# First w_ada tiles ahead of x, context reductions behind the image's, scale and shift on GpSimd, in a hybrid attention and convolution layer

## The chip, the cores and the metric

The kernel runs on one core of one Trainium2 chip. A core has a matrix engine (TensorE, PE in the profile), a vector engine (VectorE, DVE), an activation engine (ScalarE, ACT), a general engine (GpSimd, POOL) and an engine that mostly issues transfers (SyncE, SP). Each runs its own list of instructions in order, and they wait for each other by semaphores. The metric is the time of one execution on the device in microseconds, lower is better. The kernel before took 1092.82 us in the median of three runs (1089.09 to 1093.6).

## The reference

The layer takes 1024 latent tokens x and 256 context tokens ctx of width 1024. The change lies in the first lines, the modulation:

```python
def modulate(x, cond, norm_g, w_ada, b_ada):
    shift, scale, gate = jnp.split(jax.nn.silu(cond) @ w_ada + b_ada, 3, axis=-1)
    return rms_norm(x, norm_g) * (1 + scale) + shift, gate

def hybrid_layer(x, xc, c, c_ctx, lp, update_ctx):     # update_ctx is False: one layer
    h, gate = modulate(x, c, ...)                      # image: conditioned on c
    hc, gate_c = modulate(xc, c_ctx, ...)              # context: conditioned on c_ctx
    z = h @ lp['w_in']                                 # 1024 x 8704
    kc, vc = na_kv(hc @ lp['w_in'][:, A_K:A_Z], ...)   # keys and values of the context
    q, k, v = ...                                      # from z
    ya = neighbourhood_attention(q, k, v, kc, vc, rpb) * silu(z[A_Z])
    yb = short_conv_branch(z, ...)
    yc = conformer_branch(z, ...)
    return x + gate * merge_branches(z, ya, yb, yc, ...)
```

So each of the 1024 columns has a scale and a shift, each of them one dot product of length 1024 with a row of w_ada; one pair for the image (with silu(c)), another for the context (with silu(c_ctx)), from the same rows of w_ada. Everything is float32, and a matrix product is made as three products of rounded parts (high by high, high by low, low by high).

## The kernel before

The 1024 columns are eight blocks of 128, k = 0 to 7. Scale and shift of a block lie in A_t and B_t, one value per partition. They are made on VectorE: a tile `wada` holds 128 rows of w_ada (128 x 1024, 512 KB), and one scalar_tensor_tensor instruction multiplies it by the condition's row and adds up each partition (the function image_ada, line 399; below a *reduction*). Each block has two such tiles, one for the scale and one for the shift, sixteen in all, loaded by load_w_ada (line 346). Two small VectorE instructions then make A_t (line 401) and B_t (line 402) from the sums. The same tiles are reduced a second time with the context's condition row (ctx_ada, line 408), sixteen more reductions.

The opening of the program is one loop over k. In step k: the 384 columns of w_in for the first pair of heads are loaded (`wraw`, line 445), block k's w_ada tiles are loaded and reduced, the weights are split into a high part `wh` (ScalarE, line 450) and a low part `wl` (VectorE, line 452), and `modulated` turns tokens 0 to 511 of block k into `ha`: TensorE transposes four tiles of x into a bank of PSUM (line 371), ScalarE writes the high part with scale and shift applied (line 373) and the same unrounded as `xh` (line 376), and VectorE subtracts to get the low part (line 379). `outer` then adds block k's twelve products per four token tiles to the banks in PSUM (lines 418 to 420). Three steps later, `second` does the same for tokens 512 to 767, into `hb`. There are two banks for transposes, and a bank is free again when its `xh` is written.

x tiles are normalised in `normed`: ScalarE squares and sums (line 358), GpSimd makes the reciprocal root in two instructions (lines 80 and 81), and VectorE (line 363) or ScalarE (line 361) scales the tile. After the loop, rest_image does tokens 768 to 1023, the context's A and B are completed on GpSimd (lines 484 to 486), and context_h transposes and modulates the context tokens. The rows of the first gated unit's weights (`grow`, lines 431 to 433) are loaded and split when k reaches GATED.

Where buffers lie matters for the order. The six w_ada tiles of blocks 0 to 2 (EARLY) lie in buffers that become hb2 to hb7 later, so both reductions must have read a tile before the hb tile that takes its place is written; the table CTX_ROWS puts those six context reductions into steps 4 to 7. The other ten lie in fifteen shared row buffers (ROWS), with x, context and weight tiles.

The order of instructions on each engine is not the order of the code alone. A planner in the language lays the recorded instructions out in time by its own estimates and sorts each engine's list by that; `issue_after` holds an instruction behind another. So a change in the opening moves instructions later in the program too.

```python
def image_ada(k):
    for j in range(2):
        dve.scalar_tensor_tensor(out=junk, in0=wa[k][j], scalar=1.0, in1=sc, ..., accum_out=da[:, j : j + 1])
    dve.tensor_scalar(out=A_t[:, k, 0:1], ...)
    state["ada"] = dve.tensor_scalar(out=B_t[:, k, 0:1], ...)
```

Of the kernel before, what the change touches and what calls it, by code (L numbers as in the profile page):

```python
# [40 lines left out]
GATED = 6  # L41
CTX_AT = (8, 3, 3, 3)

CTX_ROWS = {5: 4, 4: 5, 3: 6, 2: 7, 1: 7, 0: 7}
# [3 lines left out]
def tile_hybrid(ctx: ExitStack, tc, x, xT, cx, cond, crow, ng, w_ada, b_ada, wqkv, wz,  # L48
# [234 lines left out]
    A_t = cst.tile([P, KT, 2], F32, name="A_t")  # L283
    state["vc"] = 0
    B_t = cst.tile([P, KT, 2], F32, name="B_t")
# [22 lines left out]
    with tc.tile_pool(name="st", bufs=1) as st, tc.tile_pool(name="ps_t", bufs=1, space=PSUM) as pst:  # L308
# [17 lines left out]
        cst.tile([P, KT, 2], F32, name="sig")  # L326
# [39 lines left out]
        def modulated(k, tiles, i, hi, lo, on=act, sub=dve):  # L366
# [5 lines left out]
            a, b = A_t[:, k, i : i + 1], B_t[:, k, i : i + 1]  # L372
# [11 lines left out]
        b1 = cst.tile([P, KT], F32, name="b1")  # L384
        pool.tensor_scalar(out=b1, in0=b_t[:, 8:16], scalar1=1.0, scalar2=None, op0=ALU.add)
        x0 = [load_x(x, t, four(a1.tile([P, D], F32, tag=("qT", "kT", "vb")[t], name="xt")) if t < 3 else four(row4k("xt"))) for t in range(4)]
        wa = [load_w_ada(0)]
# [7 lines left out]
        def image_ada(k):  # L395
            junk = st.tile([P, 2, 2, 256], BF16, tag="junk", name="junk", bufs=1)
            da = small[:, 20 + 2 * k : 22 + 2 * k]
            for j in range(2):
                dve.scalar_tensor_tensor(out=junk, in0=wa[k][j], scalar=1.0, in1=sc, op0=ALU.mult, op1=ALU.mult,
                                         accum_out=da[:, j : j + 1])  # L400
            dve.tensor_scalar(out=A_t[:, k, 0:1], in0=da[:, 0:1], scalar1=b1[:, k : k + 1], scalar2=ng_t[:, k : k + 1], op0=ALU.add, op1=ALU.mult)
            state["ada"] = dve.tensor_scalar(out=B_t[:, k, 0:1], in0=da[:, 1:2], scalar1=b_t[:, k : k + 1], scalar2=None, op0=ALU.add)

        def ctx_ada(i):

            k, j = i // 2, i % 2
            junk = st.tile([P, 2, 2, 256], BF16, tag="junk", name="junk", bufs=1)
            dve.scalar_tensor_tensor(out=junk, in0=wa[k][j], scalar=1.0, in1=scx, op0=ALU.mult, op1=ALU.mult, accum_out=dx[:, k, j : j + 1])
# [34 lines left out]
        for k in range(KT):  # L443
# [11 lines left out]
            with tc.issue_after(state["ada"].ins):  # L455
                for i in CTX_ROWS:
                    if CTX_ROWS[i] == k:
                        ctx_ada(i)
            if k == 1:
                x1 += [normed(load_x(x, t, four(row4k("xt"))), act) for t in (4, 5)]  # L460
            if k >= LAG:
                second(k - LAG)
            if k == GATED:
                gated.append(load_rows(wz[CGL], [a1.tile([P, 2, 256], F32R, tag="cht", name="grow", bufs=4) for _ in range(4)]))
            if k == KT - 1:
                x2 = [normed(load_x(x, t, four(row4k("xt"))), act) for t in (6, 7)]
        for k in range(KT - LAG, KT):
            second(k)
        late = [i ^ 1 for i in range(2 * KT) if i ^ 1 not in CTX_ROWS]
# [1049 lines left out]
```

## Time and profile before

| what | value |
|---|---|
| timed runs | 1092.82, 1089.09, 1093.6 us |
| the profiled execution: its own time, its span | 1091.25 us, 1089.5 us |
| TensorE busy | 1064.1 us, 98% of the span |
| VectorE, ScalarE, GpSimd busy | 760.9, 564.5, 633.8 us |
| mean granted TensorE clock | 0.992 |
| moved by DMA | 186.26 MB, mean 171 GB/s |
| image reductions (line 399) | 16, the first at 11.8, the last at 47.9 us, 1217 ns each |
| context reductions (line 408) | 16, the first at 33.6, the last at 76.6 us, 1216 ns each |

A row of an order of time gives the start in us, the duration in us, the engine, the line, the operation, the tiles written and read with their shape, and how often; in brackets the idle time of the engine before it and what ended it. "SPq" is the issue of a transfer by SyncE. PEld is the loading of weights into TensorE, which overlaps with matmuls. A row of the table by stages gives start and end, the length, the busy time of each engine with the number of instructions, the granted clock of TensorE (1.00 is full), the share of time in which the DMA engines were busy, and GB/s.

### The profile page before, as it was taken

What the parts mean: (1) busy time and instruction counts of PE and PEld (TensorE: products, weight loads), DVE (VectorE), ACT (ScalarE), POOL (GpSimd) and SP (SyncE); (2) the same over time, 40 slices, a digit from 0 to 9 for tenths busy, and PEclk for the clock granted to TensorE, in tenths of its full rate; (3) what the DMA queues carried; (4) which work ended last, traced back from release to release, by engine and by line L of the source; (5) the groups of instructions that cost most, each with busy time, mean ns of one, the idle gap of its engine ahead of it and who ended that gap; (6) DMA issues with size and microseconds to landing.
All of it is one profiled execution on the core that took longest, in us unless ns stands there. A gap on an engine that the chain in (4) does not pass through costs nothing.

```text
span 1089.5 us, 16045 instructions
## 1 busy us (share of the span) xinstructions
PE 1064.1 (98%) x5270; PEld 910.6 (84%) x5270; DVE 760.9 (70%) x1261; ACT 564.5 (52%) x1194; POOL 633.8 (58%) x660
## 2 busy tenths in 40 slices
PE   7899999999999999999999999999999999999998
PEld 5788998998999888887888888887888888888886
DVE  6985476666666654433995898997973569988664
ACT  6764676557656675665533334234445534425730
POOL 3154967427646388333998786886685461623770
PEclk7999999999999999999999999999999999999999
DMA  9627514313222346448746446555554998461372
GB/s 349 228 78 244 188 52 126 97 45 106 95 73 77 108 156 215 154 146 299 251 155 191 157 143 190 185 197 193 165 172 160 329 340 303 136 248 62 98 231 97
DMA packets 92995, 186.26 MB, mean 171 GB/s; under 512 B 11792, under 2 KB 36752, under 8 KB 92816
## 3 DMA queue, kind: packets, MB, share of 16 engines
q1 hardware_dynamic: 88304, 183.13, 50.2%
q10 hardware_dynamic: 4608, 2.10, 0.7%
q8 instruction: 42, 0.69, 0.3%
q14 instruction: 41, 0.34, 0.1%
HBM read 136.96 MB, written 50.79 MB: 172 GB/s over the span
## 4 chain that ended last, share of the span: by engine, by line
PE 74%; DMA 7%; DVE 6%; POOL 6%; issue 3%; ACT 2%; SPq 1%; ACTq 0%; POOLq 0%; DVEq 0%
PE ops L110 4%; PE ops L109 4%; PE ops L111 4%; PE qps L678 3%; PE py L635 3%; PE qps L680 3%; PE qps L679 3%; PE pp L615 3%; PE ps L111 3%; PE ps L109 3%; PE ps L110 2%; DVE cv L830 2%; DMA wada<-in_w_ada 2%; PE gd L854 2%; PE gd L855 2%
## 5 line engine op out<-in xcount | busy, mean ns | idle before, releaser
L830 DVE SCALAR_TENSOR_TENSOR cv<-upad,cf_t,cv 128x1024 f32<-128x1024 f32 x120 | 153.8, 1281 | 1.0
L92 POOL TENSOR_TENSOR wl<-wr,wh 128x384 fp32r<-128x384 f32 (+1 forms) x87 | 84.3, 977 | 68.4 <-ACT wh L90 50.7
L764 POOL TENSOR_TENSOR wl<-s,wh 128x512 fp32r<-128x512 f32 x83 | 107.8, 1311 | 17.9 <-ACT wh L763 17.8
L763 ACT CAST wh<-s 128x512 fp32r<-128x512 f32 x111 | 66.3, 610 | 99.8 <-POOL s L767 37.6
L618 DVE TENSOR_TENSOR plo<-pp,phi 128x256 fp32r<-128x256 f32 (+2 forms) x96 | 54.5, 576 | 36.2 <-ACT phi L617 35.3
L90 ACT CAST wh<-wr 128x384 fp32r<-128x384 f32 (+1 forms) x96 | 45.9, 485 | 37.9 <-PE qps L679 16.5
L678 PE MATMUL qps<-ha,wh 128*128 128x512 f32 x160 | 63.1, 396 | 1.6 <-ACT quarter L685 1.6
L679 PE MATMUL qps<-ha,wh 128*128 128x512 f32 x160 | 63.8, 398 | 0.0
L680 PE MATMUL qps<-ha,wl 128*128 128x512 f32 x160 | 62.7, 394 | 0.0
L574 POOL TENSOR_TENSOR bias<-mk,img 64x96 f32<-64x96 bf16 (+1 forms) x96 | 44.7, 472 | 26.5 <-DVE mn L600 19.3
L617 ACT CAST phi<-pp 128x256 fp32r<-128x256 f32 (+2 forms) x96 | 46.5, 495 | 20.4 <-PE pp L615 19.9
L600 DVE CUSTOM_DVE_ANT_0 pt<-sl,bias,mn 128x384 f32<-128x384 f32 (+1 forms) x64 | 37.2, 581 | 17.2 <-PE sl L597 16.2
L764 POOL TENSOR_TENSOR wl<-wro,wh 128x512 fp32r<-128x512 f32 x12 | 16.6, 1384 | 53.6 <-ACT wh L763 53.6
L615 PE MATMUL pp<-ident,pt 128*128 128x128 f32 x304 | 46.9, 272 | 0.0
L80 POOL TENSOR_SCALAR ssh<-ssh 128x4 f32<-128x4 f32 (+1 forms) x40 | 11.5, 287 | 60.5 <-DVE ssh L255 57.7
L601 ACT ACTIVATE pt<-sc,mn 128x256 f32<-128x256 f32 x64 | 30.6, 478 | 30.8 <-DVE mn L600 29.0
L615 PEld LDWEIGHTS pp<-ident,pt 128*128 128x128 f32 x304 | 37.9, 140 | 7.8 <-DVE plo L618 0.3
L81 POOL TENSOR_TENSOR ssh<-ssh,half_neg 128x4 f32<-128x4 f32 (+1 forms) x40 | 39.0, 975 | 3.0
L109 PE MATMUL ps<-wh,hb 128*128 128x384 f32 x112 | 38.8, 347 | 0.6 <-ACT rawc L224 0.5
L608 DVE TENSOR_SCALAR pt<-pt,mn 128x640 f32<-128x640 f32 (+1 forms) x64 | 38.5, 643 | 1.0
L854 PE MATMUL gd<-hb,wh 128*128 128x512 f32 x96 | 37.4, 390 | 1.7 <-DVE c L860 1.7
L111 PE MATMUL ps<-wh,hb 128*128 128x384 f32 x112 | 37.8, 342 | 0.3 <-DVE hb L379 0.3
(437 smaller groups left out, 3753.4 us busy)
## 6 DMA issues: line engine op xcount, KB each, us to landing
wr<-in_wz SPq DMA_DIRECT2D x34, 512.0 KB, 3.8
gs<-gd SPq DMA_DIRECT2D x24, 512.0 KB, 5.3
wr<-in_wz SPq DMA_DIRECT2D x52, 192.0 KB, 2.6
wada<-in_w_ada SPq DMA_DIRECT2D x16, 512.0 KB, 8.6
wrf<-in_wo SPq DMA_DIRECT2D x16, 512.0 KB, 3.5
cht<-chd SPq DMA_DIRECT2D x24, 256.0 KB, 2.9
wro<-in_wout SPq DMA_DIRECT2D x24, 256.0 KB, 4.6
p1d<-quarter SPq DMA_DIRECT2D x20, 256.0 KB, 2.8
```

The lines of the kernel that those rows point to most:

```text
L92: lo_eng.tensor_tensor(out=lo[:, :n], in0=raw[:, :n], in1=hi[:, :n].bitcast(F32), op=ALU.subtract)
L109: pe.matmul(ps, ah, bh, start=i == 0, stop=False)
L110: pe.matmul(ps, ah, bl, start=False, stop=False)
L111: pe.matmul(ps, al, bh, start=False, stop=i == n - 1)
L615: pe.transpose(out=pp[:, c * P : c * P + P], in_=src, identity=ident)
L678: pe.matmul(ps, wh, bh, start=k == 0, stop=False, skip_group_check=True)
L679: pe.matmul(ps, wh, bl, start=False, stop=False, skip_group_check=True)
L680: pe.matmul(ps, wl, bh, start=False, stop=k % 4 == 3, skip_group_check=True)
L763: act.copy(hi, src)
L764: eng.tensor_tensor(out=lo, in0=src, in1=hi.bitcast(F32), op=ALU.subtract)
L830: dve.scalar_tensor_tensor(out=acc, in0=src, scalar=cf_t[:, i, j : j + 1], in1=acc, op0=ALU.mult, op1=ALU.add)
L854: pe.matmul(ps, wh, bh, start=first and j == 0, stop=False, skip_group_check=True)
```

## The change

Three things are changed, and their surroundings with them.

- The first two w_ada tiles are loaded ahead of the first four tiles of x, instead of behind them.
- All sixteen context reductions are recorded after rest_image, held behind the last image reduction. The six tiles whose buffers become hb tiles are loaded a second time, into row buffers; the table CTX_ROWS goes. GATED is 7 instead of 6, and x tiles 6 and 7 are asked for ahead of the `grow` rows.
- A_t and B_t become one tile AB. Per block, GpSimd adds the biases to both sums and multiplies both by their factors (the scale's is the norm's weight, the shift's is 1.0), two instructions on 128x2 in place of two VectorE instructions on 128x1. The constants for it lie in the new tile `ab`. For the context, two GpSimd instructions on 128x16 replace three on 128x8. The tile `var` of a later stage moves into `small`.

```diff
-GATED = 6
+GATED = 7
-CTX_ROWS = {5: 4, 4: 5, 3: 6, 2: 7, 1: 7, 0: 7}
...
+        pool.tensor_copy(ab[:, 0, :, 1:2], b_t[:, :8].rearrange("p (k o) -> p k o", o=1))
+        pool.tensor_scalar(out=ab[:, 0, :, 0:1], in0=b_t[:, 8:16].rearrange("p (k o) -> p k o", o=1), scalar1=1.0, scalar2=None, op0=ALU.add)
+        pool.tensor_copy(ab[:, 1, :, 0:1], ng_t.rearrange("p (k o) -> p k o", o=1))
+        pool.memset(ab[:, 1, :, 1:2], 1.0)
+        wa = [load_w_ada(0)]
         x0 = [load_x(x, t, ...) for t in range(4)]
-        wa = [load_w_ada(0)]
...
             for j in range(2):
-                dve.scalar_tensor_tensor(out=junk, in0=wa[k][j], ..., in1=sc, ..., accum_out=da[:, j : j + 1])
-            dve.tensor_scalar(out=A_t[:, k, 0:1], in0=da[:, 0:1], scalar1=b1[:, k : k + 1], scalar2=ng_t[:, k : k + 1], op0=ALU.add, op1=ALU.mult)
-            state["ada"] = dve.tensor_scalar(out=B_t[:, k, 0:1], in0=da[:, 1:2], scalar1=b_t[:, k : k + 1], scalar2=None, op0=ALU.add)
+                state["ada"] = dve.scalar_tensor_tensor(out=junk, in0=wa[k][j], ..., in1=sc, ..., accum_out=da[:, j : j + 1])
+            pool.tensor_tensor(out=da, in0=da, in1=ab[:, 0, k], op=ALU.add)
+            pool.tensor_tensor(out=AB[:, 0, k], in0=da, in1=ab[:, 1, k], op=ALU.mult)
 
         def ctx_ada(i):
             k, j = i // 2, i % 2
+            if i < EARLY:
+                w = four(row4k("wada"))
+                nc.sync.dma_start(w, four(w_ada[1 - j, k]))
+            else:
+                w = wa[k][j]
...
-            with tc.issue_after(state["ada"].ins):
-                for i in CTX_ROWS:
-                    if CTX_ROWS[i] == k:
-                        ctx_ada(i)
...
-        late = [i ^ 1 for i in range(2 * KT) if i ^ 1 not in CTX_ROWS]
+        late = [*range(EARLY, 2 * KT), *range(EARLY)]
...
         rest_image()
+        with tc.issue_after(state["ada"].ins):
+            for i in late:
+                ctx_ada(i)
...
-        pool.tensor_tensor(out=A_t[:, :, 1], in0=dx[:, :, 0], in1=b1, op=ALU.add)
-        pool.tensor_tensor(out=A_t[:, :, 1], in0=A_t[:, :, 1], in1=ng_t, op=ALU.mult)
-        pool.tensor_tensor(out=B_t[:, :, 1], in0=dx[:, :, 1], in1=b_t[:, :8], op=ALU.add)
+        pool.tensor_tensor(out=dx, in0=dx, in1=ab[:, 0], op=ALU.add)
+        pool.tensor_tensor(out=AB[:, 1], in0=dx, in1=ab[:, 1], op=ALU.mult)
```

Lines of the changed kernel are a few less than before: its image reduction is line 398, its context reduction 412, the two GpSimd instructions 400 and 401, the subtraction 376, the high part 370.

Three places show how the order moves. The first is SyncE's list at the start of the program; `xt` are tiles of x. Before:

```order
L74 DMA cond_t<-in_cond 128x16
L74 DMA ng_t<-in_ng 128x8
L74 DMA b_t<-in_b_ada 128x24
L351 DMA xt<-in_x 128x1024 x4
L346 DMA wada<-in_w_ada 128x1024 x2
L445 DMA wraw<-in_wqkv 128x384 x2
```

and with the change:

```order
L72 DMA cond_t<-in_cond 128x16
L72 DMA ng_t<-in_ng 128x8
L72 DMA b_t<-in_b_ada 128x24
L343 DMA wada<-in_w_ada 128x1024 x2
L348 DMA xt<-in_x 128x1024 x4
L449 DMA wraw<-in_wqkv 128x384 x2
```

The two w_ada tiles and the four x tiles have changed places.

The second is VectorE at the last block, k = 7: `sc` is the image's condition row, `sc1` the context's, ha6 is the output of k = 6, hb3 that of the second half at k = 3. Before:

```order
L399 SCALAR_TENSOR_TENSOR junk_620,pad0_79<-wada_616,sc_200 128x1024
L379 TENSOR_TENSOR ha6_167<-xh_563,ha6_167 128x512
L399 SCALAR_TENSOR_TENSOR junk_620,pad0_79<-wada_618,sc_200 128x1024
L401 TENSOR_SCALAR A_t_175<-pad0_79,b1_217,ng_t_213 128x1
L379 TENSOR_TENSOR hb3_580<-xh_585,hb3_580 128x256
L402 TENSOR_SCALAR B_t_176<-pad0_79,b_t_215 128x1
L452 TENSOR_TENSOR wl_626<-wraw_614,wh_625 128x384
L408 SCALAR_TENSOR_TENSOR junk_650,pad0_79<-wada_304,sc1_231 128x1024
L433 TENSOR_TENSOR grow_597<-wr_610,grow_595 128x256
L408 SCALAR_TENSOR_TENSOR junk_652,pad0_79<-wada_229,sc1_231 128x1024
```

and with the change:

```order
L398 SCALAR_TENSOR_TENSOR junk_595,pad0_79<-wada_591,sc_199 128x1024
L456 TENSOR_TENSOR wl_551<-wraw_539,wh_550 128x384
L376 TENSOR_TENSOR ha6_167<-xh_560,ha6_167 128x512
L398 SCALAR_TENSOR_TENSOR junk_595,pad0_79<-wada_593,sc_199 128x1024
L376 TENSOR_TENSOR hb3_575<-xh_580,hb3_575 128x256
L412 SCALAR_TENSOR_TENSOR junk_777,pad0_79<-wada_391,sc1_232 128x1024
L437 TENSOR_TENSOR grow_655<-wr_657,grow_653 128x256
L472 TENSOR_SCALAR qg8_159<-qg_t_715 128x1
L473 TENSOR_SCALAR kgn_160<-kg_t_717 128x1
L412 SCALAR_TENSOR_TENSOR junk_779,pad0_79<-wada_393,sc1_232 128x1024
L437 TENSOR_TENSOR grow_655<-wr_661,grow_653 128x256
L412 SCALAR_TENSOR_TENSOR junk_781,pad0_79<-wada_441,sc1_232 128x1024
```

A_t and B_t are gone from the list, and the context reductions (line 412) begin only behind the last image reduction; before, three stood ahead of it.

The third is ScalarE between the output of k = 6 and that of k = 7 (ha6 and ha7). Before:

```order
L373 ACTIVATE ha6_167<-xT_ps_557,B_t_176,A_t_175 128x512
L376 ACTIVATE xh_563<-xT_ps_557,B_t_176,A_t_175 128x512
L376 ACTIVATE xh_585<-xT_ps_581,B_t_176,A_t_175 128x256
L361 ACTIVATE xt_670<-xt_670,pad0_79 128x1024
L450 CAST wh_625<-wraw_614 128x384
L432 CAST grow_595<-wr_610 128x256
L361 ACTIVATE xt_677<-xt_677,pad0_79 128x1024
L373 ACTIVATE ha7_168<-xT_ps_629,B_t_176,A_t_175 128x512
```

and with the change:

```order
L370 ACTIVATE ha6_167<-xT_ps_554,AB_175 128x512
L373 ACTIVATE xh_560<-xT_ps_554,AB_175 128x512
L370 ACTIVATE hb3_575<-xT_ps_576,AB_175 128x256
L373 ACTIVATE xh_580<-xT_ps_576,AB_175 128x256
L355 ACTIVATE sq_641,pad0_79<-xt_639 128x1024
L355 ACTIVATE sq_648,pad0_79<-xt_646 128x1024
L436 CAST grow_653<-wr_657 128x256
L370 ACTIVATE hb4_625<-xT_ps_626,AB_175 128x256
L358 ACTIVATE xt_639<-xt_639,pad0_79 128x1024
L436 CAST grow_653<-wr_661 128x256
L370 ACTIVATE ha7_168<-xT_ps_604,AB_175 128x512
```

The squares of x tiles 6 and 7 and the output hb4 now stand ahead of ha7; one of the two scalings and the cast of the weights stand behind it.

More of the change, by code (lines that the diff above doesn't have):

```diff
@@ L282, in tile_hybrid @@
     a1 = a1ctx.enter_context(tc.tile_pool(name="a1", bufs=1))
-    A_t = cst.tile([P, KT, 2], F32, name="A_t")
+    AB = cst.tile([P, 2, KT, 2], F32, name="AB")
     state["vc"] = 0
-    B_t = cst.tile([P, KT, 2], F32, name="B_t")
     def glu(i):
@@ L325, in tile_hybrid @@
         cond_t = const(cond, [P, KT, 2], "cond_t")
-        cst.tile([P, KT, 2], F32, name="sig")
+        ab = cst.tile([P, 2, KT, 2], F32, name="ab")
         act.activation(cond_t, cond_t, AF.Silu)
@@ L371, in modulated @@
                 pe.transpose(out=pt[:, j * P : (j + 1) * P], in_=xt[:, k // 4, k % 4 // 2, k % 2 * P : k % 2 * P + P], identity=ident)
-            a, b = A_t[:, k, i : i + 1], B_t[:, k, i : i + 1]
+            a, b = AB[:, i, k, 0:1], AB[:, i, k, 1:2]
             act.activation(hi, pt[:, :n], AF.Identity, bias=b, scale=a)
@@ L398, in image_ada @@
             for j in range(2):
[L399 to L402, printed above, removed]
+                state["ada"] = dve.scalar_tensor_tensor(out=junk, in0=wa[k][j], scalar=1.0, in1=sc, op0=ALU.mult, op1=ALU.mult,
+                                                        accum_out=da[:, j : j + 1])
+            pool.tensor_tensor(out=da, in0=da, in1=ab[:, 0, k], op=ALU.add)
+            pool.tensor_tensor(out=AB[:, 0, k], in0=da, in1=ab[:, 1, k], op=ALU.mult)
         def ctx_ada(i):
             k, j = i // 2, i % 2
+            if i < EARLY:
[3 more added lines that the diff above has]
+                w = wa[k][j]
             junk = st.tile([P, 2, 2, 256], BF16, tag="junk", name="junk", bufs=1)
-            dve.scalar_tensor_tensor(out=junk, in0=wa[k][j], scalar=1.0, in1=scx, op0=ALU.mult, op1=ALU.mult, accum_out=dx[:, k, j : j + 1])
+            dve.scalar_tensor_tensor(out=junk, in0=w, scalar=1.0, in1=scx, op0=ALU.mult, op1=ALU.mult, accum_out=dx[:, k, j : j + 1])
         image_ada(0)
@@ L1251, in norm_steps @@
         yield from col_sums(square, sums)
-        var = cst.tile([P, KT], F32, name="var")
+        var = small[:, :KT]
         for b in range(2):
```

9 lines of the change are left out of this document (2 added, 7 removed).

## The prediction

> **What bounds the kernel now.** The table by stages was read first, to see where TensorE is not the bound; then, inside the stage that has idle time, the order of time on VectorE, ScalarE and GpSimd, and the queue of SyncE for when tiles land.
>
> ```profile
> PE 1064.1 (98%) x5270; PEld 910.6 (84%) x5270; DVE 760.9 (70%) x1261; ACT 564.5 (52%) x1194; POOL 633.8 (58%) x660
> ```
>
> ```profile
> core 0: us, PE busy (x) PEld busy (x) DVE busy (x) ACT busy (x) POOL busy (x), PEclk, DMA share, GB/s
> 17.00:34.00 17.00, 15.49 (x73) 14.06 (x74) 15.42 (x34) 13.04 (x22) 2.86 (x4) 0.82 1.03 401
> 34.00:51.20 17.20, 13.63 (x72) 12.07 (x70) 17.20 (x39) 12.92 (x25) 3.74 (x5) 0.90 0.56 188
> 51.20:67.00 15.80, 14.50 (x75) 12.77 (x76) 13.86 (x31) 12.53 (x27) 9.41 (x11) 1.00 0.42 144
> 67.00:85.00 18.00, 17.45 (x103) 15.56 (x102) 13.79 (x33) 9.87 (x22) 6.47 (x12) 1.00 0.03 8
> 120.00:1089.50 969.50, 959.69 (x4726) 818.95 (x4724) 674.76 (x1088) 488.49 (x1043) 582.77 (x579) 1.00 0.50 165
> ```
>
> From 120 us on TensorE is busy 959.7 of 969.5 us, so nothing the change does can be won or lost there but by the order of that work. The change acts in the opening. From 17 to 67 us TensorE idles 1.5 + 3.6 + 1.3 = 6.4 us, and VectorE is the bound: 17.20 of 17.20 us busy between 34 and 51.2. TensorE's granted clock is 0.82 and 0.90 there; after a gap of 2.04 us it ran at half pace:
>
> ```profile
> 39.63 0.45 PE L418 MATMUL ps<-wh,ha 128*128 128x384 f32 x1 [2.04 <-ACT ha L373]
> 39.91 0.34 PE L419 MATMUL ps<-wl,ha 128*128 128x384 f32 x1
> 40.31 0.52 PE L419 MATMUL ps<-wl,ha 128*128 128x384 f32 x1
> 43.67 0.34 PE L419 MATMUL ps<-wl,hb 128*128 128x384 f32 x1
> ```
>
> Between 40.31 and 43.67 matmuls start 0.32 us apart instead of 0.17: about 1.7 us lost. The ceiling of the change is so about 6.4 + 1.7 = 8 us.
>
> The last of the eight steps (k = 7) on VectorE:
>
> ```profile
> 44.90 1.22 DVE L408 SCALAR_TENSOR_TENSOR junk<-wada,sc 128x1024 bf16<-128x1024 f32 x1
> ...
> 46.17 1.22 DVE L399 SCALAR_TENSOR_TENSOR junk<-wada,sc 128x1024 bf16<-128x1024 f32 x1
> 47.31 0.08 DVE L399 DVE_READ_ACCUMULATOR junk<-wada,sc 128x1 f32 x1
> 47.31 0.69 DVE L379 TENSOR_TENSOR ha<-xh,ha 128x512 fp32r<-128x512 f32 x1
> 47.92 1.22 DVE L399 SCALAR_TENSOR_TENSOR junk<-wada,sc 128x1024 bf16<-128x1024 f32 x1
> 49.06 0.27 DVE L401 TENSOR_SCALAR A_t<-pad,b,ng_t 128x1 f32<-128x1 f32 x1
> 49.25 0.42 DVE L379 TENSOR_TENSOR hb<-xh,hb 128x256 fp32r<-128x256 f32 x1
> 49.58 0.21 DVE L402 TENSOR_SCALAR B_t<-pad,b_t 128x1 f32<-128x1 f32 x1
> 49.70 0.55 DVE L452 TENSOR_TENSOR wl<-wraw,wh 128x384 fp32r<-128x384 f32 x1
> ```
>
> Starts count, since durations overlap: a reduction holds VectorE 1.15 us, the 512-wide subtraction 0.6, the 256-wide 0.34, A_t 0.19, B_t 0.12, wl 0.48. The tile that L399 reads at 47.92 had long landed: SyncE holds eight transfers, and an issue starts when the one eight before it has landed. The second tile of k = 7 stands eight ahead of cs_t:
>
> ```profile
> 6.10 1.43 SPq L346 DMA_DIRECT2D wada<-in_w_ada  x2
> ...
> 11.05 0.33 SPq L445 DMA_DIRECT2D wraw<-in_wqkv  x1
> 12.36 0.83 SPq L346 DMA_DIRECT2D wada<-in_w_ada  x2
> ...
> 38.78 0.33 SPq L74 DMA_DIRECT2D cs_t<-in_cs  x1
> ```
>
> So it was there by 38.8. By the same rule x tile 0 landed by 6.10 and the two first w_ada tiles by 11.05 and 12.36, five tiles after it: 1.25 us a tile.
>
> **The two w_ada tiles ahead of x.** They now land by about 7.2, the four x tiles by 8.6 to 12.4, two slots (2.5 us) later. ScalarE squares x as it lands:
>
> ```profile
> 11.12 1.06 ACT L358 ACTIVATE sq<-xt 128x1024 bf16<-128x1024 f32 x1
> ...
> 16.16 0.78 ACT L373 ACTIVATE ha<-xT_ps,B_t,A_t 128x512 fp32r<-128x512 f32 x1 [2.26 <-DVE B_t L402]
> ```
>
> The last square starts after three others (1.05 each) and two copies of scx (0.5 each) from 8.6 on: 12.75 instead of 11.12. Behind it come GpSimd's root, VectorE's scaling, the transposes; then k = 0's first output, which before waited for B_t until 16.16 and no longer does. I carry VectorE's first free moment for k = 1 from 16.44 to 17.25 (+0.8) and the first output from 16.16 to 17.65 (+1.5).
>
> **A and B on GpSimd.** VectorE loses eight times 0.19 + 0.12 = 2.5 us of work. But each pair now crosses to GpSimd and back as two dependent operations, and GpSimd does not work freely beside VectorE:
>
> ```profile
> 58.15 1.21 DVE L408 SCALAR_TENSOR_TENSOR junk<-wada,sc 128x1024 bf16<-128x1024 f32 x1
> 58.33 1.10 POOL L80 TENSOR_SCALAR ssh<-ssh 128x4 f32<-128x4 f32 x1 [3.02 <-DVE ssh L255]
> ...
> 62.34 0.20 POOL L80 TENSOR_SCALAR ssh<-ssh 128x4 f32<-128x4 f32 x1
> ...
> 76.25 0.21 POOL L486 TENSOR_TENSOR B_t<-pad,b_t 128x8 f32<-128x8 f32 x1 [2.51 <-DVE junk L408]
> ```
>
> The same L80 takes 0.20 us alone and 1.10 under a reduction, ending when it ends. So each of the pair costs 0.2 at best and up to 1.2 behind the VectorE instruction in flight; the pair 0.5 to 2.4, where B_t was there 0.3 after the reduction. The price is paid where VectorE must wait for the result, at the ha subtraction: pair, then ScalarE's ha and xh (1.4 us). By the new order, filled with these durations, VectorE waits about 1.9 us at k = 1 and at k = 2 (there also for ScalarE, whose scaling of x tiles 4 and 5 needs roots that are held up the same way) and 0.5 each at k = 4 and 5: 4.9, against 1.4 before. I take the blocked value, since VectorE is busy nearly all the time; bounds are 2.3 and 6.5.
>
> A rule of the Trainium skill speaks against this part: "GPSIMD Engine Reference", Specifications, says GpSimd shares its SBUF interfaces with VectorE and contends with instructions that have two SBUF inputs or run in a two-port mode; the reductions and subtractions are such, and the trace agrees (1.10 us against 0.20). By that rule the sum is the one with 4.9 us of waits; without it, 2.3.
>
> **Context rows behind the image's.** Three context reductions (3 x 1.15 = 3.45 us) leave the stretch before the last image reduction, and with GATED = 7 three grow subtractions (1.0). Sum on VectorE at the end of the last image reduction, 49.14 before: -2.5 - 3.45 - 1.0 + (4.9 - 1.4) + 0.8 = -2.65, so 46.5.
>
> **What is late next.** That gain does not reach k = 7's output. ScalarE's order now puts two squares of x tiles 6 and 7 (1.05 each), one scaling (1.1), two grow casts (0.35), and three 256-wide outputs (0.46) ahead of it: 5.25 us after k = 6's xh, which ends at 44.9. And GpSimd's pair for k = 7 stands behind x tile 6's root, which two context reductions hold up. Both give 50.2 to 50.4:
>
> ```profile
> 47.55 1.16 ACT L361 ACTIVATE xt<-xt,pad 128x1024 f32<-128x1024 f32 x1
> ...
> 50.35 0.77 ACT L373 ACTIVATE ha<-xT_ps,B_t,A_t 128x512 fp32r<-128x512 f32 x1
> ...
> 51.18 0.44 PE L418 MATMUL ps<-wh,ha 128*128 128x384 f32 x1 [0.83 <-ACT ha L373]
> ```
>
> On TensorE: it comes to its wait for k = 7 at about 49.75 instead of 51.18 (-1.4), with four matmuls and two transposes of k = 4's second half done that came later before (-0.9). It then waits some 3.1 us in all for k = 7's output and for subtractions queued behind three context reductions, where 1.95 were lost before (+1.15). Further on the hb7 subtraction stands behind nine context reductions and comes at 61.0, when TensorE stands at 59.3 (+1.7). Sum: -1.4 - 0.9 + 1.15 + 1.7 = +0.55.
>
> **The context itself.** After the last image reduction VectorE has 16 context reductions ahead instead of 13 and ends them at about 78.5:
>
> ```profile
> 76.56 1.20 DVE L408 SCALAR_TENSOR_TENSOR junk<-wada,sc 128x1024 bf16<-128x1024 f32 x1
> ...
> 78.25 0.26 POOL L485 TENSOR_TENSOR A_t<-A_t,ng_t 128x8 f32<-128x8 f32 x1
> ...
> 79.45 0.56 ACT L373 ACTIVATE ch<-xT_ps,B_t,A_t 128x256 fp32r<-128x256 f32 x1
> ```
>
> Before, they ended at 77.7, A was there at 78.5 and first used at 79.45. Now it is there at 79.3 to 79.7: I add nothing, bound +1. The **six reloads** are 3 MB, 7.5 us at 1.25 a tile; they fall where the DMA engines idle and are read as the last six reductions, from 66 us on; cover gone, they would cost up to those 7.5:
>
> ```profile
> 45.00:55.00 10.00, 7.67 (x42) 6.40 (x41) 9.63 (x21) 9.59 (x17) 3.26 (x4) 1.00 0.21 66
> ```
>
> In SyncE's queue they stand ahead of the context x and w1raw loads, needed near 63 and 68. The merged tiles and var in small cost nothing.
>
> **Sum.** The profiled execution took 1091.25, its span 1089.5; the three timed runs were 1092.82, 1089.09 and 1093.6. The mean of the four is 1091.7; plus 0.5 gives 1092.2 as the time of a run: no change. (A measurement of this kernel tells about 0.5%, 5.4 us, from no change.)
>
> **Rivals.** *Faster: the relief of VectorE goes through.* If the pairs slip in between VectorE's instructions, waits are 2.3 (-2.6), the later x costs nothing (-1.5), hb7's wait (-1.7) and the 1.15 vanish: 1092.2 - 7 = 1085.2. For it: VectorE is the full bound from 34 to 51 us, and two operations of 0.2 us are cheap. Against: rows of 1.10, and ScalarE's new order. Chance 0.21.
>
> *Slower: the context becomes late.* Sixteen reductions now follow the image, six of them on tiles that SyncE issues only once a row buffer is free, in turn with other loads. The output pairs of the context occupy both transposing banks, so TensorE stops once A and B come later than about 79.5, one for one. With the reloads' 7.5 us uncovered by half, and one more slow stretch of the clock (1.7) at a gap over 2 us: 1092.2 + 3.8 + 1.7 = 1097.7. Against: 20 us between the issue and the first use. Chance 0.13.
>
> *The order of the rest decides.* The planner also rearranges the work after 120 us; TensorE idles 9.8 us there, and half of it more or less would be 1087 or 1097. For: the rows of later stages do differ. Against: TensorE is 99% busy in any order. Chance 0.08, half each way.
>
> *The reloads or the new order do not do what they say:* the forecast then stands anyway.
>
> **How the numbers follow.** Forecast 0.58, faster 0.21, slower 0.13, order 0.08. Some of the forecast's own spread (1088 to 1096) and of the rivals lies inside 0.5%. Faster 0.22, same 0.61, slower 0.17. The range must reach toward 1085 and toward 1098: 1085 to 1098.5 leaves out about 2 in 10.
>
> **What would show it.** Right: the last image reduction ends near 46.5, k = 7's output stays near 50.4, GpSimd's pairs show operations of about 1 us, TensorE waits at hb4 and hb7, TensorE's idle time from 17 to 85 us stays within 2 us of before. Wrong: k = 7's output before 48 (the pairs are cheap, or ScalarE is freer), context A after 82, or TensorE's idle time after 120 us off by more than 3 us.

## The result, and the profile after

The changed kernel took 1085.06 us in the median of seven runs (1083.6 to 1087.99), the kernel before beside it 1091.28 (seven runs, 1087.82 to 1093.6): a ratio of 0.9949, with a 95% interval of 0.9933 to 0.9965. Measured again later, twelve runs against twenty of the kernel before on one chip, it was 0.9961 (0.9947 to 0.9975), 1084.85 against 1089.30. So the change makes the kernel 4 to 6 us faster, at the edge of what I had called no change. The forecast of 1092.2 was too high, mostly by a gain that lies where the forecast had put nothing. One run of the kernel context_only below took 1182.59 us at a granted clock of 0.846, where its others show 0.99; it does not count in that kernel's median, 1088.17.

The profiled execution of the changed kernel is the slowest of its seven runs (1087.99 us, span 1086.2), so its span is only 3.3 us shorter than that of before. Its page begins:

```profile
PE 1063.0 (98%) x5270; PEld 910.3 (84%) x5270; DVE 768.6 (71%) x1245; ACT 563.5 (52%) x1194; POOL 646.2 (59%) x678
```

The table by stages of the changed kernel, with the same stages as in the prediction:

```profile
core 0: us, PE busy (x) PEld busy (x) DVE busy (x) ACT busy (x) POOL busy (x), PEclk, DMA share, GB/s
17.00:34.00 17.00, 12.25 (x53) 10.78 (x54) 13.49 (x22) 11.34 (x18) 6.84 (x11) 0.77 1.03 405
34.00:51.20 17.20, 15.85 (x96) 14.57 (x95) 16.18 (x34) 14.00 (x26) 6.38 (x12) 1.00 0.58 201
51.20:67.00 15.80, 15.29 (x73) 13.34 (x74) 14.83 (x32) 12.35 (x27) 5.74 (x8) 0.89 0.92 320
67.00:85.00 18.00, 17.69 (x100) 15.45 (x99) 14.87 (x33) 11.16 (x25) 12.33 (x15) 1.00 0.05 15
120.00:1086.20 966.20, 958.42 (x4728) 819.45 (x4726) 684.72 (x1088) 487.70 (x1044) 584.98 (x580) 1.00 0.48 165
```

The first stage lost (TensorE 12.25 us busy against 15.49, 53 products against 73), the second won it back (15.85 against 13.63, 96 products against 72, with the clock at 1.00 against 0.90). TensorE's idle time over the four stages from 17 to 85 us is 6.9 us before and after. VectorE is no longer the full bound: 16.18 of 17.20 instead of 17.20. After 120 us the stage is 3.3 us shorter: TensorE idles 7.8 us instead of 9.8, and is busy 1.3 us less (958.42 against 959.69).

The rows that answer the prediction's, on VectorE, ScalarE, GpSimd and TensorE of the changed kernel in order of time:

```profile
45.60 1.22 DVE L398 SCALAR_TENSOR_TENSOR junk<-wada,sc 128x1024 bf16<-128x1024 f32 x1
```

```profile
18.51 0.78 ACT L370 ACTIVATE ha<-xT_ps,AB 128x512 fp32r<-128x512 f32 x1 [2.95 <-PE xT_ps L368]
...
50.19 0.78 ACT L370 ACTIVATE ha<-xT_ps,AB 128x512 fp32r<-128x512 f32 x1
```

```profile
31.84 1.06 POOL L401 TENSOR_TENSOR AB<-pad,ab 128x2 f32<-128x2 f32 x1
...
39.88 0.26 POOL L401 TENSOR_TENSOR AB<-pad,ab 128x2 f32<-128x2 f32 x1
...
47.30 1.41 POOL L79 TENSOR_TENSOR pad<-pad,half_neg 128x1 f32<-128x1 f32 x1
48.68 0.22 POOL L400 TENSOR_TENSOR pad<-pad,ab 128x2 f32<-128x2 f32 x1
48.98 1.18 POOL L401 TENSOR_TENSOR AB<-pad,ab 128x2 f32<-128x2 f32 x1
```

```profile
51.69 1.15 PE L368 MATMUL xT_ps<-ident,xt 128*128 128x128 f32 x4 [1.81 <-ACT xh L373]
```

The last image reduction ends at 46.82 (forecast 46.5, before 49.14). The output of k = 7 starts at 50.19 (forecast 50.2 to 50.4, before 50.35): GpSimd's pair for k = 7 stands behind the root of an x tile, as forecast, and its second operation is stretched to 1.18 us. The first output of all comes at 18.51, later than the forecast 17.65.

Where is the gain, then? The first scores of the attention (the matmuls that write `sl`) mark the end of the opening, the last of them the end of the attention. The view of one source line gives the first and the last start (before, then after):

```profile
L596 PE MATMUL sl<-ks,qd x64: 278/334/443, 114.0 to 475.9; 128*128 128x384 f32 x48, 128*128 128x256 f32 x16
```

```profile
L595 PE MATMUL sl<-ks,qd x64: 277/334/442, 114.3 to 473.7; 128*128 128x384 f32 x48, 128*128 128x256 f32 x16
```

The opening, the only place that the change touches in the code apart from `var`, ends 0.3 us later. The attention takes 359.4 us instead of 361.9. The 2.5 us lie behind the opening, in code that was not changed, only ordered anew.

### The profile page after: what moved, and what is told of

Read it like the earlier page. It is cut to its first block, busy times and chain, and to the rows that moved or that the text cites. A ratio compares the mean times of both kernels' runs of the same rounds, so it can differ in the third digit from the quotient of the medians.

```text
span 1086.2 us, 16054 instructions
## 1 busy us (share of the span) xinstructions
PE 1063.0 (98%) x5270; PEld 910.3 (84%) x5270; DVE 768.6 (71%) x1245; ACT 563.5 (52%) x1194; POOL 646.2 (59%) x678
## 4 chain that ended last, share of the span: by engine, by line
PE 80%; DVE 3%; DMA 1%; POOL 1%; issue 1%; ACT 1%; SPq 0%; ACTq 0%; POOLq 0%; DVEq 0%
PE ops L109 4%; PE ops L107 4%; PE ops L108 4%; PE qps L677 3%; PE qps L678 3%; PE qps L679 3%; PE gd L853 3%; PE gd L855 3%; PE gd L854 3%; PE py L634 3%; PE pp L614 3%; PE ps L107 2%; PE ps L109 2%; PE ps L108 2%; PE ge L855 2%; PE gc L855 2%
## 5 line engine op out<-in xcount | busy, mean ns | idle before, releaser
L79 POOL TENSOR_TENSOR ssh<-ssh,half_neg 128x4 f32<-128x4 f32 (+1 forms) x40 | 43.1, 1078 | 2.9
L607 DVE TENSOR_SCALAR pt<-pt,mn 128x640 f32<-128x640 f32 (+1 forms) x64 | 44.0, 728 | 1.0
```

## The experiments

**Theory and rival.** Theory: the opening is about even, and the gain comes from the planner's other order of the rest. Rival: the three edits bring it themselves, by relieving VectorE.

Comparing the two lists instruction by instruction showed how the orders differ. From the first scores on, the kernel before and the changed kernel part at one place: one pair of VectorE instructions, near 132 us, has changed places. Behind it the lists are sorted differently, TensorE's from 135 to 525 us and VectorE's to 563 us of the kernel before; from there to the end they are the same again, so "the rest" is in fact the attention and a little beyond it. Other small edits of the opening give one of the same two orders of the rest, call them B (as before) and A (as after). So the order could be switched by one edge on that pair with the opening untouched.

### before_pair_swapped and after_pair_swapped

```diff
 # before_pair_swapped: the kernel before, order A
-    def norm(ps, dst, n):
+    def norm(ps, dst, n, after=None):
...
-        dve.tensor_tensor(out=dst..., op=ALU.mult)
+        with tc.issue_after(after) if after else ExitStack():
+            dve.tensor_tensor(out=dst..., op=ALU.mult)
...
-                norm(raw[:, :256], tm, 4)
+                norm(raw[:, :256], tm, 4, state["mn"][1].ins if (hp, t) == (1, 1) else None)
...
-            dve.tensor_reduce(out=mn[:, 0:2], in_=sc, axis=AX.X, op=ALU.min)
+            state.setdefault("mn", []).append(dve.tensor_reduce(out=mn[:, 0:2], in_=sc, axis=AX.X, op=ALU.min))
```

> The kernel before, with one NoSync edge: VectorE's third scaling of raw q and k rows of the second head pair (L257, at 132.46 us in the profile before) is queued behind the row minimum of the second pair of query blocks (L589, at 132.80) and so changes places with it. Nothing ahead of 132 us is touched. From there on the planner's order is that of the changed kernel. Theory (the gain lies in the order of the rest): 1085 to 1086 us, 5 to 6 below the kernel before, with the first scores' matmul still at 117.4. Rival (the three edits of the opening bring it themselves): the opening is unchanged, so 1090 to 1092, no change.

```diff
 # after_pair_swapped: the changed kernel, order B
+        if before:      # the row minimum is queued behind this scaling
+            tc.add_manual_dep(before, tm.ins.name, mybir.DependencyInfo(mybir.DependencyClass.NoSync, mybir.DependencyReason.DATA))
```

> The changed kernel, with one NoSync edge that puts the same two VectorE instructions into the order of the kernel before (the scaling first, then the row minimum). The opening with all three edits is untouched. From there on the order is that of the kernel before. Theory (order of the rest): the gain is lost, 1091 to 1092.5, with the first scores' matmul still at 117.7. Rival (the opening brings it): 1085 to 1086, as the changed kernel.

Measured beside a kernel before of 1089.32 us: the kernel before with order A took 1085.20, a ratio of 0.9972 (0.9960 to 0.9984); the changed kernel with order B took 1087.77, 0.9989 (0.9974 to 1.0004). (The matmul at 117.4 and 117.7 us of the two expectations is the second product of the first scores, not the first one, at 114.0 and 114.3.) With the second measurement of the changed kernel:

> The changed kernel once more, unaltered, beside the runs of the kernel before on the same chip. The pair swapped in the kernel before gave 0.9972 and the three edits with the order of before 0.9989. Theory (the order of the rest gives about 3 us, the opening about 1, and they add): 0.996, 1084.5 to 1086 where before is 1089 to 1090. Rival (they do not add: the order alone is the gain): 0.997. Rival (something else in the changed kernel gives more): 0.995 or less, as in its first comparison.

0.9961 (0.9947 to 0.9975) is just the product of 0.9972 and 0.9989. So the order of the rest is worth 0.28%, 3.0 us (1.7 to 4.4 by the interval), measured directly with the old opening and as the quotient of two comparisons with the new one. The three edits in the opening are worth 0.11%, 1.2 us, which the interval does not tell from nothing. The theory had the right place and too large a share (it expected 5 to 6 us of the order, and 1091 to 1092.5 for the changed kernel with order B); the rival is wrong for the larger part.

What the pair does, on VectorE of the kernel before and of the kernel before with the pair swapped:

```profile
129.83 1.28 DVE L551 TENSOR_TENSOR qlz<-qT,qd 64x1024 fp32r<-64x1024 f32 x1
132.46 0.43 DVE L257 TENSOR_TENSOR tm<-raw,ssh 128x256 f32<-128x256 f32 x1 [1.35 <-POOL ssh L81]
132.80 0.69 DVE L589 TENSOR_REDUCE mn<-sc 128x2 f32<-128x512 f32 x1
```

```profile
130.43 1.28 DVE L552 TENSOR_TENSOR qlz<-qT,qd 64x1024 fp32r<-64x1024 f32 x1
131.74 0.69 DVE L590 TENSOR_REDUCE mn<-sc 128x2 f32<-128x512 f32 x1
133.07 0.43 DVE L258 TENSOR_TENSOR tm<-raw,ssh 128x256 f32<-128x256 f32 x1 [0.64 <-POOL ssh L81]
```

Before, VectorE stands 1.35 us in front of a scaling that needs GpSimd's root, with a row minimum ready behind it. Swapped, the minimum fills that wait. From the end of `qlz` to the end of the pair that saves 0.6 us; but the planner lays out all that follows from there, and the other layout keeps TensorE fuller: from 180 to 240 us it is busy 58.94 of 60 us before, and 60.00 with the pair swapped. Over the whole of 120 to 480 us it idles 2.0 us before and 0.5 with the pair swapped. That is 1.5 of the 3.6 us by which the attention is shorter; the other 2.1 us, in which TensorE counts as busy, were not traced.

```profile
180.00:240.00 60.00, 58.94 (x368) 55.90 (x367) 37.91 (x93) 32.96 (x92) 25.80 (x40) 1.00 0.29 93
```

```profile
180.00:240.00 60.00, 60.00 (x387) 57.68 (x386) 42.36 (x97) 36.18 (x98) 30.26 (x42) 1.00 0.30 95
```

The attention's length sorts all profiled executions whose large tiles lie where they lay before by their order: 361.9, 361.1 and 361.0 us with B, 358.0 to 359.5 in seven with A. (First and last start of `sl` for the two swapped kernels:)

```profile
L597 PE MATMUL sl<-ks,qd x64: 277/334/420, 114.6 to 472.9; 128*128 128x384 f32 x48, 128*128 128x256 f32 x16
```

```profile
L597 PE MATMUL sl<-ks,qd x64: 277/334/442, 113.7 to 474.8; 128*128 128x384 f32 x48, 128*128 128x256 f32 x16
```

### The edits one by one

context_only is the kernel before with the third edit alone (GATED stays 6; the planner gave it order A by itself):

```diff
-            with tc.issue_after(state["ada"].ins):
-                for i in CTX_ROWS:
-                    if CTX_ROWS[i] == k:
-                        ctx_ada(i)
...
+            if i < EARLY:
+                w = four(row4k("wada"))
+                nc.sync.dma_start(w, four(w_ada[1 - j, k]))
...
         rest_image()
+        with tc.issue_after(state["ada"].ins):
+            for i in late:
+                ctx_ada(i)
```

> The kernel before with one of the three edits: the context's rows behind the last image columns, six tiles loaded twice. x is still asked for first, scale and shift stay on VectorE, the rows of wz are asked for where they were. The planner gives its rest the order of the changed kernel. Theory (order of the rest): 1085 to 1086.5, the whole gain from this edit alone. Rival (relief of VectorE and of the start add up over the three edits): 1088 to 1090, about half, since two of the three are left out.

Measured: 1088.17, 0.9997 (0.9983 to 1.0012). The theory was wrong; the median lies in the rival's range, but half of the gain, the rival's reason, is not there. The kernel has the order that alone brings 3.0 us, and no gain: beside that order without it, the edit costs some 2.7 us.

The other two edits together, first as they came (A and B as in the diff of the change, `wa = [load_w_ada(0)]` ahead of x0, but with `var` in a tile of its own):

> The kernel before with the other two edits: the first two tiles of w_ada ahead of x, and scale and shift made on GpSimd. The context's rows stay where they were. The planner leaves the rest in the order of the kernel before. Theory (order of the rest): 1090.5 to 1092.5, no change or a little slower. Rival (the opening's relief): 1088 to 1090, faster by the 2.5 us of VectorE's work that these two take away.

Measured: 1112.0, a ratio of 1.0217 (1.0195 to 1.0239), outside of everything expected. Most of it was an accident of memory, below; with `var` moved into `small`, as the changed kernel has it,

```diff
-        var = cst.tile([P, KT], F32, name="var")
+        var = small[:, :KT]
```

> The two edits that took 1112 us (w_ada's first tiles ahead of x, scale and shift on GpSimd, context rows where they were), with one line more, which the changed kernel has too: the variances of the last norm lie in the columns of small instead of 32 bytes of their own. Without that line the pool of small constants is 32 bytes longer per partition and every large tile behind it starts 32 bytes further on. Theory (the 32 bytes cost the 22 us): 1088 to 1091, no change against before. Rival (the two edits cost it themselves, by the opening that ended 8 us late): 1108 to 1113.

it took 1094.41, 1.0045 (1.0027 to 1.0062). So 17.6 us of the 1112.0 were the place of the tiles, and 0.45%, 4.9 us, is what the two edits do cost. The first scores come at 118.7 instead of 114.0, and the place is k = 7 (GpSimd, TensorE, and the stage on TensorE of this kernel):

```profile
51.42 0.19 POOL L80 TENSOR_SCALAR pad<-pad 128x1 f32<-128x1 f32 x1 [1.54 <-ACT sq L357]
51.69 1.04 POOL L402 TENSOR_TENSOR pad<-pad,ab 128x2 f32<-128x2 f32 x1
52.69 0.76 POOL L81 TENSOR_TENSOR pad<-pad,half_neg 128x1 f32<-128x1 f32 x1
53.42 0.79 POOL L403 TENSOR_TENSOR AB<-pad,ab 128x2 f32<-128x2 f32 x1
```

```profile
55.35 0.69 PE L419 MATMUL ps<-wh,ha 128*128 128x384 f32 x1 [3.83 <-ACT ha L372]
```

```profile
51.00:67.00 16.00, 12.17 (x51) 11.02 (x51) 13.47 (x29) 11.66 (x25) 7.25 (x11) 0.79 0.50 160
```

The last reduction for k = 7 ends at 51.05; the pair that makes its scale and shift is mixed in GpSimd's list with the root of an x tile, all of it under VectorE's context reductions, and ends at 54.2. TensorE waits 3.83 us, and its granted clock in that stage is 0.79, where it was 1.00 in the same stretch before. That is the loss the prediction described for scale and shift on GpSimd, with the context's reductions still in front; in the change those reductions are gone and the last pair ends at 50.16. How much of the 4.9 us the later x takes was not tried with the context in front.

Then the changed kernel with one or both of these two edits taken back, order A and the places of the tiles held the same:

```diff
 # after_x_first: the changed kernel
-        wa = [load_w_ada(0)]
         x0 = [load_x(x, t, ...) for t in range(4)]
+        wa = [load_w_ada(0)]
```

> The changed kernel with x asked for ahead of w_ada's first two tiles again, as before; context rows behind, scale and shift on GpSimd, the order of the rest and the places of the large tiles as in the changed kernel (1084.85 beside 1089.3). Theory (x two tiles later costs the opening its 1.5 to 2.3 us at the first output, of which part arrives at the first scores' matmul): 1083 to 1084.5. Rival (the first w_ada tiles early let the reductions start early, and that is worth what x loses): 1084.5 to 1086.

```diff
 # after_scale_on_vector: the changed kernel, and the edge of before_pair_swapped
-            pool.tensor_tensor(out=da, in0=da, in1=ab[:, 0, k], op=ALU.add)
-            pool.tensor_tensor(out=AB[:, 0, k], in0=da, in1=ab[:, 1, k], op=ALU.mult)
+            dve.tensor_scalar(out=A_t[:, k, 0:1], in0=da[:, 0:1], scalar1=b1[:, k : k + 1], scalar2=ng_t[:, k : k + 1], op0=ALU.add, op1=ALU.mult)
+            state["ada"] = dve.tensor_scalar(out=B_t[:, k, 0:1], in0=da[:, 1:2], scalar1=b_t[:, k : k + 1], scalar2=None, op0=ALU.add)
```

> The changed kernel with scale and shift made on VectorE again, eight pairs of 0.27 and 0.20 us; w_ada's first tiles early, context rows behind; the order of the rest is held to that of the changed kernel by the one NoSync edge, and the large tiles lie where they lay. Theory (on GpSimd the last pair queues behind the row factors of x6 and x7 and is stretched under VectorE's reductions, which costs as much as VectorE saves): 1083.5 to 1085.5, no difference. Rival (relief of VectorE by 2.5 us shortens the opening): 1086.5 to 1088.

context_late_only_same_order has both of these edits:

> The changed kernel with both taken back: x first, scale and shift on VectorE. What is left of the change is the context's rows behind the image's with six tiles loaded twice, and the rows of wz asked for one round later; the order of the rest is that of the changed kernel. Theory (the context's rows behind are the only part of the opening that gains, the other two together cost 5 us where the context's rows stay in front): 1081 to 1084, the best so far. Rival (the opening is worth nothing either way, as the context's rows alone without the later wz rows gave no gain): 1085 to 1086, as with the swapped pair alone.

| kernel | edits in the opening | order | first scores, us | attention, us | median, us | ratio to before |
|---|---|---|---|---|---|---|
| before | none | B | 114.0 | 361.9 | 1088.2 to 1091.3 | 1 |
| before_pair_swapped | none | A | 114.6 | 358.3 | 1085.20 | 0.9972 |
| context_only | context | A | 114.9 | 358.3 | 1088.17 | 0.9997 |
| context_late_only_same_order | context, wz rows a round later | A | 115.3 | 359.5 | 1088.21 | 0.9997 (0.9979 to 1.0015) |
| after_scale_on_vector | context, wz, x later | A | 116.3 | 358.0 | 1088.13 | 0.9992 (0.9975 to 1.0008) |
| after_x_first | context, wz, GpSimd | A | 114.9 | 358.0 | 1086.07 | 0.9973 (0.9956 to 0.9989) |
| after_again | all | A | 113.1 | 358.3 | 1084.85 | 0.9961 |
| after_pair_swapped | all | B | 113.7 | 361.1 | 1087.77 | 0.9989 |
| x_late_scale_gpsimd_same_layout | x later, GpSimd | B | 118.7 | 361.0 | 1094.41 | 1.0045 |

My expectation that the context's move alone would be the best kernel fell, and so did the one that scale and shift on GpSimd are a draw. Moving the context back costs 2.7 us against the same order without it; putting scale and shift on GpSimd then wins 3.4 (0.9992 to 0.9961, measured on two chips), and 2.6 with x first and both kernels on one chip (0.9997 to 0.9973, at the edge of the noise); with the context in front the same edit, together with the later x, loses 4.9. x later is 0.9961 against 0.9973 without it, not to be told from nothing; the gain expected of x first did not show. None of these kernels measured better than the changed one.

Why the context's move may cost, and GpSimd cover it: the six reloads stand in SyncE's list ahead of the two context tiles, which are issued from 57.76 us on in the changed kernel, instead of at 48.74 and 55.90. ScalarE meets the first square of a context tile and stands before it (the kernel before, after_scale_on_vector, after_again):

```profile
59.65 1.06 ACT L358 ACTIVATE sq<-xt 128x1024 bf16<-128x1024 f32 x1 [0.90 <-DMA xt<-in_cx]
```

```profile
61.58 1.06 ACT L357 ACTIVATE sq<-xt 128x1024 bf16<-128x1024 f32 x1 [2.36 <-DMA xt<-in_cx]
```

```profile
62.34 1.06 ACT L355 ACTIVATE sq<-xt 128x1024 bf16<-128x1024 f32 x1 [2.81 <-DMA xt<-in_cx]
```

Behind that square stand the outputs that TensorE needs. Where scale and shift are on VectorE, TensorE runs dry (after_scale_on_vector, TensorE's order of time and two stages):

```profile
64.97 0.45 PE L107 MATMUL ps<-wh,hb 128*128 128x384 f32 x1 [0.72 <-ACT hb L372]
66.67 0.44 PE L370 MATMUL xT_ps<-ident,xt 128*128 128x128 f32 x2 [0.50 <-ACT xh L375]
67.73 0.68 PE L370 MATMUL xT_ps<-ident,xt 128*128 128x128 f32 x2 [0.62 <-DVE xh L377]
69.68 0.69 PE L182 MATMUL psq<-ident,tm 128*128 128x128 f32 x2 [1.26 <-ACT raw L173]
```

```profile
57.00:80.00 23.00, 19.90 (x93) 17.12 (x93) 20.21 (x43) 12.40 (x26) 16.66 (x19) 0.85 0.36 137
...
66.00:72.00 6.00, 3.62 (x14) 2.81 (x14) 5.30 (x13) 4.61 (x10) 4.79 (x6) 0.65 0.07 22
```

It is busy 19.90 of 23 us from 57 to 80, at a clock of 0.85. With all three edits (after_again) ScalarE's wait is as long, and TensorE is busy 22.15 of 23, at a clock of 1.00:

```profile
57.00:80.00 23.00, 22.15 (x119) 19.41 (x119) 21.64 (x48) 15.02 (x32) 15.57 (x18) 1.00 0.40 144
```

The reading that fits is that TensorE, held up more before 34 us, still has work in hand when ScalarE stands. That the late context tiles are the cause was not tried by itself (asking for them ahead of the reloads would be the run), and context_only speaks against it as the whole cause. TensorE runs dry there as well:

```profile
57.00:80.00 23.00, 18.77 (x100) 15.62 (x99) 18.96 (x42) 12.47 (x26) 13.81 (x18) 1.00 0.37 136
```

In before_pair_swapped it is busy 22.60 of these 23 us. Yet the first scores of context_only come only 0.3 us later and its attention is as long; the other 2.7 us by which its profile is longer arise between 713 and 920 us, where both kernels have the same list and TensorE of context_only waits for VectorE four times (0.44, 0.38, 0.51 and 0.55 us), that of before_pair_swapped not once. The first of these waits is 1.59 and 2.45 us in the two profiles of the changed kernel, so a profile alone does not give it to the edit. Where the 3.0 us between the two medians come from stays open.

### Where the tiles lie

```diff
 # before_32_bytes_on, before_64_bytes_on, before_128_bytes_on: 2, 3 and 5 times KT columns
-        var = cst.tile([P, KT], F32, name="var")
+        var = cst.tile([P, 2 * KT], F32, name="var")[:, :KT]
```

> The kernel before with nothing changed but 32 bytes more behind the variances' tile: the large tiles that follow (ha, hb, T, the shared tiles of the attention) start 32 bytes further on, the weights' tiles at the other end stay where they are. Every engine's order is that of before. Theory (layout costs): the 128x512 matmuls' mean goes from 389 to 395 ns and the time to 1104 to 1113. Rival (the edits cost it): 1088 to 1091, no change, matmuls at 389.

> The same with 64 bytes more, so that the large tiles start 64 bytes further on than in the kernel before. If the cost hangs on the place within 64 bytes, this is the kernel before again: 1088 to 1091, matmuls at 389 ns. If any displacement from the place of before costs: 1100 or more. If a displacement of either kind does nothing: 1088 to 1091 here and with 32 bytes.

> The kernel before with 128 bytes more behind the variances' tile; the large tiles start 128 bytes further on, every order is that of before. 32 bytes on gave 1106.4 and 64 bytes on 1102.1, beside 1089.3. If what costs is the place within 128 bytes, this is the kernel before again: 1087 to 1091, the 128x512 matmuls at 389 ns. If the distance to the weights' tiles, which stay where they are, or the sum of all places matters: 1098 or more, matmuls at 392 ns or more.

Every instruction list is that of the kernel before; only the large tiles start further on. Measured: 1106.37, 1.0146 (1.0116 to 1.0177); 1102.09, 1.0112 (1.0086 to 1.0138); 1103.36, 1.0135 (1.0111 to 1.0160). So any of the three displacements costs 12 to 17 us by the medians, and neither 64 nor 128 bytes brings the old pace back. One stage of 100 us, full of 512-wide products (before, then 32, 64 and 128 bytes on):

```profile
620.00:720.00 100.00, 100.00 (x443) 82.82 (x442) 91.65 (x98) 35.86 (x61) 79.82 (x65) 1.00 0.51 169
```

```profile
620.00:720.00 100.00, 100.00 (x430) 80.34 (x429) 92.56 (x99) 37.60 (x63) 80.74 (x66) 1.00 0.52 174
```

```profile
620.00:720.00 100.00, 100.00 (x439) 82.05 (x438) 93.87 (x100) 37.77 (x63) 82.35 (x70) 1.00 0.50 173
```

```profile
620.00:720.00 100.00, 100.00 (x432) 81.13 (x431) 91.47 (x99) 38.10 (x62) 80.45 (x66) 1.00 0.50 166
```

TensorE is busy without a gap in all four, at a granted clock of 1.00, and gets through 443, 430, 439 and 432 products. Their starts are 226.7, 233.3, 228.9 and 232.4 ns apart in the mean (before, the 443 start between 619.79 and 719.98).

With 32 and with 128 bytes this pace is most of the loss: behind the attention, where the 512-wide products are, the profiles are 12.5 and 10.3 us longer. With 64 bytes it is only 3.2 us there, and 9.1 us lie in the attention, which takes 371.0 us instead of 361.9:

```profile
L596 PE MATMUL sl<-ks,qd x64: 274/337/458, 112.3 to 483.2; 128*128 128x384 f32 x48, 128*128 128x256 f32 x16
```

TensorE waits there 3.89 us at 407 and 2.03 us at 429 us, for VectorE instructions that took many times their usual length (last section).

The changed kernel's products keep the old pace because its merged tiles add 32 bytes to the pool of constants and `var` in `small` takes 32 away.

## Why the prediction was right or wrong

*What bounds the kernel*: right. VectorE was the bound from 34 to 51.2 us and is not any more.

*w_ada ahead of x*: mis-sized. The first output came 2.35 us later, not 1.5: ScalarE's first square began at 9.37 us, when its x tile had landed, not at 8.6. As a part of the whole it cost nothing that could be measured.

*A and B on GpSimd*: the mechanism was right, its size somewhat too large. The operations take 0.2 to 0.26 us where they are free and up to 1.18 where VectorE holds them, but only three of the sixteen took over 1 us. VectorE waited 1.57, 1.72 and 0.77 us at the ha subtractions, 4.06 in all against 4.9. That the last image reduction ends at 46.82 against 46.5 is in part luck: these waits were 0.8 us shorter, and VectorE began k = 1 at 17.80, 0.55 us later than forecast. What the working lacked is that this part has no price of its own: with the context's reductions in front it costs (with the later x) 4.9 us, without them it is worth 3.4.

*What is late next*: right for k = 7's output (50.19) and for a wait on TensorE behind it, which was 1.81 us where 3.1 were put down in all; the 1.7 us at the hb7 subtraction did not come. The sum of +0.55 for the opening stands against +0.3 in the pair of profiles and -1.2 (+0.4 to -2.8) by the measured ratio.

*The context itself*: "I add nothing" held, though scale and shift came at 80.9, not at 79.3 to 79.7; TensorE is busy 17.69 of 18 us there, so it did not stop one for one from 79.5 on, as the second rival had it. Of the reloads the prediction said that they fall where the DMA engines idle, and noted that they stand ahead of the context's loads without a price for it. With them ScalarE waits 2.8 us instead of 0.9. In the full change that was covered; in the experiments that move the context without GpSimd's part TensorE ran dry.

*The merged tiles and var in small*: they cost nothing, as said, but only both together. The prediction took `var` for tidying; without that line the large tiles would have lain 32 bytes further on, which cost 17 to 18 us in each of the two kernels in which it was tried.

*The sum*: this is the step that failed. It took the time after 120 us as given and added the opening's 0.5 to it. The third rival, the order of the rest, was the one that decided; its size was estimated as half of TensorE's 9.8 idle us, 4.9, and it measured 3.0; its chance of 0.08 was far too low. Its sign, idle time after 120 us off by more than 3 us, was too coarse to show it: it moved by 2.0, and TensorE's busy time by 1.3. The argument against it, that TensorE is 99% busy in any order, was no argument, since 1% is twice the bound of 0.5%. Half of what should have been known could be read beforehand: the lists of before and after part at one VectorE pair, and the trace of before shows a wait of 1.35 us just there, with ready work behind it. Which of two orders is the faster one could not be read from it. Of the 7.1 us between the forecast and the first median, 3.0 are the order, 1.7 the opening (1.2 gained, 0.5 that the sum added) and 0.4 the base of the sum (1091.7 where the median of before came to 1091.28); the 2.0 that are left lie within the interval of the first comparison. That the time lies within 1085 to 1098.5 is luck: 1085.06 is just inside, the later median of 1084.85 just outside, and the lower end was put there for a relief of VectorE that did not bring the gain.

## What to carry to other kernels

Where a planner sorts the instructions, an edit anywhere is also a draw of a new order for much that follows: compare the lists, find the first pair that parts, and switch that pair alone before crediting the edit with the gain. Parts of an edit that share queues are not additive, so take them back one at a time from the whole and not only put them in one at a time. When a test changes the size of a small buffer, hold the places of the large ones, or the test measures these. Profile one kernel twice before a difference of a microsecond between two profiles is given to an edit: the two profiles of the changed kernel differ by 1.2 us at the first scores alone.

## What the runs showed of the hardware that was not expected

The place of a matrix product's operands in memory changes its pace by up to 3%, with no wait in any list: 226.7 ns from start to start against 233.3 when the large tiles lie 32 bytes further on, and 228.9 and 232.4 at 64 and 128 bytes. No rule was found; the weights' tiles stayed where they were, so the distance between the operands changed as well as their own place. "TensorE: Matmul & The Clock Gate" of the Trainium skill (Part 1) gives 215.7 ns from start to start for 512 columns at the full clock; no layout here reached that.

A short wait on TensorE can cost twice, but need not. In after_scale_on_vector, after waits of 0.72, 0.50 and 0.62 us, the granted clock was 0.50 from 68 to 74.5 us; beside the wait of 3.83 us shown above it was 0.79 over a stage of 16 us. In context_only waits of 0.72, 0.98, 0.50 and 1.54 us between 63 and 72 us left it at 1.00. The changed kernel shows both: behind the same wait for k = 7's `xh`, 1.81 and 1.80 us long, the clock fell in one profiled execution and not in the other (after, then after_again):

```profile
51.00:57.00 6.00, 5.29 (x21) 4.61 (x22) 6.00 (x13) 5.59 (x12) 1.79 (x2) 0.72 0.92 295
```

```profile
50.00:56.00 6.00, 4.71 (x26) 3.88 (x26) 6.00 (x13) 6.00 (x14) 1.87 (x2) 1.00 0.93 295
```

GpSimd can perhaps also hold VectorE. In the profiled run of the kernel with 64 bytes more, a scaling that takes 0.55 us in the median took 8.01, and a subtraction that takes 0.69 took 5.67:

```profile
398.94 8.01 DVE L608 TENSOR_SCALAR pt<-pt,mn 128x512 f32<-128x512 f32 x1
...
422.77 5.67 DVE L747 TENSOR_TENSOR hb<-hb 128x512 fp32r<-128x512 f32 x1 [1.85 <-ACT hb L746]
```

Beside each of them GpSimd worked without a gap, and each ended just after GpSimd paused, at 406.9 and 428.4 us (GpSimd's rows around the two ends):

```profile
399.32 1.72 POOL L92 TENSOR_TENSOR wl<-wr,wh 128x384 fp32r<-128x384 f32 x2
...
405.67 0.99 POOL L92 TENSOR_TENSOR wl<-wr,wh 128x384 fp32r<-128x384 f32 x1
411.10 0.74 POOL L92 TENSOR_TENSOR wl<-wr,wh 128x256 fp32r<-128x256 f32 x1 [4.44 <-ACT wh L90]
...
426.62 1.27 POOL L715 TENSOR_TENSOR hsum<-hsum 128x512 f32<-128x512 f32 x1
428.48 1.28 POOL L715 TENSOR_TENSOR hsum<-hsum 128x512 f32<-128x512 f32 x1 [0.59 <-DMA td<-hsum]
```

That the two share their way to the memory is what the Trainium skill says in "GPSIMD Engine Reference", Specifications; these rows fit it. They do not show it, since no run changes GpSimd's work alone. A busy GpSimd is also not enough: in the other thirteen profiles the same two instructions took at most 1.59 and 1.46 us. TensorE waited 3.89 and 2.03 us for them.
